# Stacked keys with doubled queries, a 128-row pool product, and the feed-forward output in groups of 2, 4, 8 and 8 tiles

## The chip, the cores and the metric

The kernel runs on one core of one Trainium2 chip. The metric is the time of one execution on the device in microseconds (us); three runs of the kernel before gave 3009.57, 3010.11 and 3011.67 us, and their median is 3010.11 us. A core has a matrix engine (PE, with its weight loads shown apart as PEld), a vector engine (DVE), a scalar engine (ACT), GpSimd (POOL) and a queue engine (SP). In this kernel SP and POOL also issue the DMA transfers.

## The reference, cut to what matters

Two layers over 1024 positions of 1024 channels. Each layer is a mixing part and a feed-forward part.

```
h    = rmsnorm(x) ; proj = h @ w_in -> q, k, v, forget logits, conv inputs, pool input px, 3 gates
qh,kh= rmsnorm per head (8 heads of 64) ; c = cumsum(log sigmoid(forget logits))
logits[t,s] = qh[t].kh[s] / 8 + c[t] - c[s], causal ; a = softmax(logits) @ v ; y_attn = a @ w_attn_out
y_conv = short_conv(...) @ w_conv_out
y_pool = per group g of 4:  d_g (64 channels) @ pool_w[g] (64 x 256), times a scale
x    = x + (g0*y_attn + g1*y_conv + g2*y_pool) @ w_o
h    = rmsnorm(x) ; gt, up = split(h @ w_ffn_in) ; x = x + (silu(gt)*up) @ w_ffn_out     (2816 hidden channels)
```

All values are float32. The kernel keeps the precision with a high and a low part for each operand, and most products take three matmuls: high by high, high by low, low by high.

## The kernel before, in words

Everything is held transposed: channels on the 128 partitions, positions along the row, in two halves of 512 positions (`n` = 0, 1). A product tile is 128 channels by 512 positions in one PSUM bank. `mm3` (lines 226 to 228) issues the three matmuls for every 128 input channels. The code is written as units in a queue (`plan`); a scheduler then sets the order of instructions of every engine from priorities and dependences, and puts in the waits. Each engine works through its list in that order.

**Attention.** Heads go in four pairs `p`; a pair's 128 channels are head `e`=0 on partitions 0 to 63 and head `e`=1 on 64 to 127. `qk_evac` and `scale_one` (lines 502 to 567) turn a product of q or k into the operands of the scores. For q of head 0 there is `qa`: the high part on rows 0 to 63, the low part on rows 64 to 127 (`qb` for head 1, mirrored). For k there are `ka` and `kb` (the high part of one head, written twice, on both halves of the rows) and `kl` (the low parts of both heads, each on its own half). `scores` (lines 648 to 684) runs over the blocks of 128 queries, `i` = 0 to 7, and both heads. A block has 128(i+1) keys, in chunks of at most 512. Each chunk takes two matmuls:

```
T.matmul(qk, lhsT=qs[:, tb],  rhs=kh[:, c0:c1],          start=True,  stop=False)   # line 669, 128 rows
T.matmul(qk, lhsT=qs[er, tb], rhs=d["kl"][er, c0:c1],    start=False, stop=True)    # line 670, 64 rows
```

DVE then adds the bias and takes the running maximum (line 676), ACT takes exp (line 681), DVE scales (line 683). One step later PE turns the block (`turn`, line 694), ACT and DVE split it into high and low (lines 697, 698), and one step after that PE multiplies by the values (line 711). Between these, `fill` puts steps of other products of `plan`: gates, and q, k and v of the next pairs. The bias rows of a pair, `negcb`, are loaded by SP (line 644) into 6 buffers, 4 per pair.

**Merge.** `merge_unit` (lines 914 to 950) makes 16 outputs of 20 matmuls per layer: 12 for attention, 6 for convolution, 2 for pooling (lines 933 and 934). The pooled input `pd` has the high part of a group on its own 64 rows and the low part on the other 64; the weight is loaded onto both halves. Line 933 multiplies all 128 rows by the weight's high part, line 934 the 64 high rows by the weight's low part.

**Feed-forward.** The 22 tiles of hidden channels are made by plain units (two tiles) and by `strassen_unit` (20 tiles), seven products of four channel tiles for each pair of tiles. Each finished tile is split into `ah` and `al` and stored to memory (lines 998, 999). The output product reads them back: `load_act` loads the tiles of a list `order` into 28 places, which are the operand tiles of the Strassen products, in the order in which those are read for the last time; each load waits until its place is free. `GROUPS` cuts the 22 tiles into three groups of 8, 8 and 6; in each group the product goes over 8 output tiles `m` and 2 halves `n`, and DVE adds the result to `x` (line 1167); the products go round seven PSUM banks (`dbank`). In group 0, `x` is loaded from memory (`load_x`, line 971, SP) just ahead of each output. `x`, `ah`, `al` and the temporaries share a ring of 18 tiles. The weights of one unit are 128 output channels wide; `load` (lines 107 to 129) brings them in on SP, ACT makes the high part (line 122), DVE the low (line 123), with 2 raw buffers and 3 split ones.

Of the kernel before, what the change touches and what calls it, by code (L numbers as in the profile page):

```python
# [9 lines left out]
F32 = mybir.dt.float32  # L10
F32R = mybir.dt.float32r
AF = mybir.ActivationFunctionType
ALU = mybir.AluOpType
# [17 lines left out]
FB = DFF // P  # L31
EPS = 1e-6
NEG = -1.0e30
GROUPS = [(0, 8), (8, 8), (16, 6)]
RING = 18
LOOK = 2
FINE = 4
# [18 lines left out]
def trunk_kernel(ctx: ExitStack, tc: tile.TileContext, x, norm_mix_g, w_in, forget_b, q_norm_g, k_norm_g,  # L56
# [158 lines left out]
    def dbank():  # L215
        tags = dense_tags[0]
        t = tags[dense_at[0] % len(tags)]
        dense_at[0] += 1
        return ps.tile([P, HN], F32, tag=t, name="dps", bufs=2 if t in ("qk", "pt") else 1)

    def mm3(dst, ws, rs, start=True, stop=True, again=False):

        n = len(ws)
        for k in range(n):
            (wh, wl), (rh, rl) = ws[k], rs[k]
            T.matmul(dst, lhsT=wh, rhs=rh, start=start and k == 0, stop=False, skip_group_check=again)  # L226
            T.matmul(dst, lhsT=wh, rhs=rl, start=False, stop=False, skip_group_check=again)  # L227
            T.matmul(dst, lhsT=wl, rhs=rh, start=False, stop=stop and k == n - 1, skip_group_check=again)  # L228
# [211 lines left out]
    for l in range(L):  # L440
# [49 lines left out]

        def pair_tiles(p):
            d = heads.setdefault(p, {})
            for nm in ("ka", "kb", "kl"):
                d[nm] = ap.tile([P, S], F32R, tag=nm, name=f"{nm}{p}", bufs=2)

        def v_tile(p):
# [49 lines left out]
        def scale_one(p, which, n, qf, r):  # L546
            d = heads[p]
            cols = slice(n * HN, (n + 1) * HN)
            gcol = (gqs if which == "q" else gk)[:, l:l + 1]
            V.scalar_tensor_tensor(out=qf, in0=qf, scalar=gcol, in1=r, op0=ALU.mult, op1=ALU.mult)  # L550
            lo, hi = slice(0, HD), slice(HD, P)
            if which == "q":
                qa = ap.tile([P, HN], F32R, tag="qa", name="qa", bufs=3)
                qb = ap.tile([P, HN], F32R, tag="qb", name="qb", bufs=3)
                A.copy(out=qa[lo], in_=qf[lo])
                A.copy(out=qb[hi], in_=qf[hi])
                V.tensor_tensor(out=qa[hi], in0=qf[lo], in1=qa[lo].bitcast(F32), op=ALU.subtract)
                V.tensor_tensor(out=qb[lo], in0=qf[hi], in1=qb[hi].bitcast(F32), op=ALU.subtract)
                d["qa", n], d["qb", n] = qa, qb
            else:  # L560
                A.copy(out=d["ka"][lo, cols], in_=qf[lo])
                A.copy(out=d["kb"][hi, cols], in_=qf[hi])
                A.copy(out=d["ka"][hi, cols], in_=qf[lo])
                A.copy(out=d["kb"][lo, cols], in_=qf[hi])
                V.tensor_tensor(out=d["kl"][lo, cols], in0=qf[lo], in1=d["ka"][lo, cols].bitcast(F32),
                                op=ALU.subtract)
                V.tensor_tensor(out=d["kl"][hi, cols], in0=qf[hi], in1=d["kb"][hi, cols].bitcast(F32),
                                op=ALU.subtract)

        v_dram = dr.tile([P, 2, KT, P], F32R, tag="vd", name="vd")  # L570

# [67 lines left out]
        def load_negc(p):  # L639
            for c in range(NH):  # L640
                for e in range(2):
                    hrow = negc_dram[2 * p + e:2 * p + e + 1, :]
                    t = ap.tile([P, HN], F32, tag="negcb", name="negcb", bufs=6)
                    nc.sync.dma_start(out=t, in_=hrow[:, c * HN:(c + 1) * HN].broadcast_to([P, HN]))
                    negc[p, e, c] = t

# [4 lines left out]
        def scores(ch):  # L651

            p, i, e = ch
            d = heads[p]
            qs, kh = (d["qa", i // 4], d["ka"]) if e == 0 else (d["qb", i // 4], d["kb"])
            tb = slice(i % 4 * P, (i % 4 + 1) * P)
            er = slice(e * HD, (e + 1) * HD)
            n_s = (i + 1) * P
            lg = ap.tile([P, S], F32, tag="lg", name="lg", bufs=3)
            mx = ap.tile([P, 6], F32, tag="mx", name="mx", bufs=4)  # L660
            nm = ap.tile([P, P], F32, tag="nm", name="nm", bufs=3)
            dg = i % 4 * P
            G.affine_select(out=nm, in_=negc[p, e, i // 4][:, dg:dg + P], pattern=[[-1, P]], compare_op=ALU.is_ge,
                            fill=NEG, base=0, channel_multiplier=1)
            top = -3.0e38
            at = 0
            for c, c0, c1 in chunks(i):
                qk = ps.tile([P, HN], F32, tag="qk", name="qk", bufs=2)
                T.matmul(qk[:, 0:c1 - c0], lhsT=qs[:, tb], rhs=kh[:, c0:c1], start=True, stop=False)  # L669
# [242 lines left out]
        def merge_unit(mm):  # L912
            specs = [wspec(w_attn_out[l], (0, 512), mm * 2 * P, 2 * P)]

            def run(w):
# [7 lines left out]
                for m in (2 * mm, 2 * mm + 1):  # L923
                    g = m // 2
                    c2 = slice(m % 2 * P, (m % 2 + 1) * P)
                    c4 = slice(m % 4 * P, (m % 4 + 1) * P)
                    rows = slice((g % 2) * HD, (g % 2 + 1) * HD)
# [41 lines left out]
        def load_x(m, n):  # L969
            xt[m, n] = ring("x")  # L970
            nc.sync.dma_start(out=xt[m, n], in_=xs[m, n])
# [182 lines left out]
        def ffo_unit(g, m, halves, before=None):  # L1154
            j0, nj = GROUPS[g]
            last = g == len(GROUPS) - 1

            def run(w):
                wh, wl = w[0]
                if before:  # L1160
                    before()
                for n in halves:
                    if g == 0:
                        load_x(m, n)
                    b = dbank()
                    mm3(b, [(wh[:, k, :], wl[:, k, :]) for k in range(nj)], [act[j0 + k, n] for k in range(nj)])
                    V.tensor_tensor(out=xt[m, n], in0=b, in1=xt[m, n], op=ALU.add)  # L1167
                    if last and l < L - 1:
                        square_acc(nq, m, n, xt[m, n])
                    yield  # L1170
            return Unit([wspec(wfo, (j0 * P, (j0 + nj) * P), m * P, P)], run)

        for n in range(NH):
            for m in range(KT):
# [32 lines left out]
        for g in range(len(GROUPS) - 1):  # L1207
            for m in range(KT):
                before = None
                if g == 0 and m == 0:  # L1210
                    before = lambda: load_act(20, 28)
                elif g == 1 and m == 0:
                    before = lambda: load_act(28, 44)
                plan.append(ffo_unit(g, m, range(NH), before))
        prefetch()
        run_tail()
        wx_stack.close()
# [63 lines left out]
```

## Time and profile before

| | |
|---|---|
| median of three runs | 3010.11 us |
| the profiled execution | 3009.41 us |
| its span, first to last instruction | 3007.6 us, mean granted clock 0.995 |
| PE busy | 2975.6 us (99%), 13680 matmuls |
| DVE busy | 1723.1 us (57%) |
| ACT busy | 1224.8 us (41%) |
| DMA | 353.83 MB, 118 GB/s over the span |

A row of the timeline gives an instruction's start and its duration. Matmuls overlap: one that lasts 0.39 us starts 0.23 us after the one before it, so the time that a matmul takes from PE is read from start to start, not from its duration. The shape "64\*128 64x512" is a matmul over 64 rows into 128 columns of weights with 512 moving columns. What stands in brackets at a row's end is idle time before it and what ended it.

### The profile page before, as it was taken

The numbers are of one execution on the slowest core, as the hardware profiler recorded it, in microseconds if no ns is written. First come the engines' busy times: TensorE is split into PE (matmuls) and PEld (weight loads), VectorE is DVE, ScalarE is ACT, GpSimd is POOL, SyncE is SP. The second block draws the span as 40 slices with busy tenths as digits, with TensorE's granted clock in tenths as the row PEclk, the third lists the DMA queues.
The fourth block names the chain that finished last, engine by engine and source line by source line (L and its number), as shares of the span: only waits on it lengthen the run. The fifth ranks groups of instructions, "written<-read, shape, count | busy, mean of one in ns | idle before, by whom it ended". The sixth has DMA issues, their size and how long they took to land.

```text
span 3007.6 us, 36474 instructions
## 1 busy us (share of the span) xinstructions
PE 2975.6 (99%) x13680; PEld 2408.9 (80%) x13680; DVE 1723.1 (57%) x3133; ACT 1224.8 (41%) x1935; POOL 426.9 (14%) x756
## 2 busy tenths in 40 slices
PE   8999999999999999999999999999999999999999
PEld 7778777887888888788887887788778888887887
DVE  7776765438585555422577667544476855653223
ACT  6666653222454444300367567432224443442002
POOL 3101111000411111321211111110003111114200
PEclk9999999999999999999999999999999999999999
DMA  5222223235533333763421231232355333338623
GB/s 170 74 77 82 73 83 105 69 107 160 189 98 112 112 112 112 231 202 115 129 84 60 74 93 63 91 116 74 107 168 176 99 112 112 110 109 266 194 63 119
DMA packets 348889, 353.83 MB, mean 118 GB/s; under 512 B 26376, under 2 KB 263432, under 8 KB 348456
## 3 DMA queue, kind: packets, MB, share of 16 engines
q1 hardware_dynamic: 281864, 208.80, 23.1%
q0 software_dynamic: 66848, 142.70, 14.7%
q8 instruction: 107, 1.75, 0.2%
q14 instruction: 70, 0.57, 0.1%
HBM read 252.81 MB, written 98.63 MB: 117 GB/s over the span
## 4 chain that ended last, share of the span: by engine, by line
PE 91%; DVE 5%; DMA 2%; issue 1%; ACT 1%; POOL 0%; SPq 0%; DVEq 0%; ACTq 0%; POOLq 0%
PE dps L226 27%; PE dps L227 26%; PE dps L228 26%; PE qk L670 2%; PE pv L711 2%; PE pt L694 2%; PE qk L669 2%; PE dps L602 1%; PE dps L604 1%; PE dps L603 1%; DVE hf L1033 1%; DVE t L232 1%; DVE hf L292 1%; DMA wr<-in_w_in_dram 1%; DMA acl<-acd 1%
## 5 line engine op out<-in xcount | busy, mean ns | idle before, releaser
L226 PE MATMUL dps<-hh,wh 128*128 128x512 f32 x1408 | 572.3, 407 | 0.0
L227 PE MATMUL dps<-hl,wh 128*128 128x512 f32 x1408 | 552.5, 393 | 1.5 <-DVE hl L232 1.1
L228 PE MATMUL dps<-hh,wl 128*128 128x512 f32 x1408 | 551.3, 392 | 0.0
L122 ACT CAST wh<-wr 128x1024 fp32r<-128x1024 f32 (+1 forms) x200 | 203.4, 1017 | 693.0 <-PE dps L227 610.1
L123 DVE TENSOR_TENSOR wl<-wr,wh 128x1024 fp32r<-128x1024 f32 (+1 forms) x200 | 240.3, 1201 | 209.6 <-ACT wh L122 209.0
L226 PEld LDWEIGHTS dps<-hh,wh 128*128 128x128 f32 x1408 | 265.7, 189 | 62.5 <-issue 12.1
L228 PEld LDWEIGHTS dps<-hh,wl 128*128 128x128 f32 x1408 | 265.3, 188 | 57.9
L227 PEld LDWEIGHTS dps<-hl,wh 128*128 128x128 f32 x1408 | 265.9, 189 | 47.3 <-DVE hl L232 1.5
L227 PE MATMUL dps<-acl,wh 128*128 128x512 f32 x704 | 277.2, 394 | 7.2 <-DMA acl<-acd 7.0
L226 PE MATMUL dps<-ach,wh 128*128 128x512 f32 x704 | 277.0, 394 | 2.7 <-DMA ach<-acd 2.6
L228 PE MATMUL dps<-ach,wl 128*128 128x512 f32 x704 | 275.8, 392 | 1.3 <-DVE wl L123 1.3
L1167 DVE TENSOR_TENSOR x<-dps,x 128x512 f32<-128x512 f32 x96 | 66.3, 691 | 333.1 <-PE dps L228 311.0
L226 PE MATMUL dps<-t,wsh 128*128 128x512 f32 x640 | 249.2, 389 | 0.0
L227 PE MATMUL dps<-t,wsh 128*128 128x512 f32 x640 | 249.0, 389 | 0.0
L228 PE MATMUL dps<-t,wsl 128*128 128x512 f32 x640 | 249.0, 389 | 0.0
L226 PE MATMUL dps<-hh,wsh 128*128 128x512 f32 x480 | 187.0, 390 | 0.9 <-ACT p L1114 0.9
L228 PE MATMUL dps<-hh,wsl 128*128 128x512 f32 x480 | 186.7, 389 | 0.0
L227 PE MATMUL dps<-hl,wsh 128*128 128x512 f32 x480 | 186.7, 389 | 0.0
L227 PEld LDWEIGHTS dps<-acl,wh 128*128 128x128 f32 x704 | 133.0, 189 | 38.6 <-DMA acl<-acd 11.7
L226 PEld LDWEIGHTS dps<-ach,wh 128*128 128x128 f32 x704 | 132.9, 189 | 34.2 <-DMA ach<-acd 7.1
L228 PEld LDWEIGHTS dps<-ach,wl 128*128 128x128 f32 x704 | 133.3, 189 | 28.8 <-DVE wl L123 1.7
L1077 DVE TENSOR_TENSOR wsl<-wr,wsh 128x1024 fp32r<-128x1024 f32 x80 | 76.2, 953 | 117.7 <-ACT wsh L1076 117.7
(263 smaller groups left out, 5461.6 us busy)
## 6 DMA issues: line engine op xcount, KB each, us to landing
wr<-in_w_in_dram SPq DMA_DIRECT2D x88, 512.0 KB, 3.8
wr<-in_w_ffn_in_dram SPq DMA_DIRECT2D x40, 1024.0 KB, 5.2
acd<-ah POOLq DMA_DIRECT2D x88, 256.0 KB, 2.3
acd<-al POOLq DMA_DIRECT2D x88, 256.0 KB, 2.5
acl<-acd POOLq DMA_DIRECT2D x88, 256.0 KB, 7.5
ach<-acd POOLq DMA_DIRECT2D x88, 256.0 KB, 7.1
td<-tg POOLq DMA_DIRECT2D x80, 256.0 KB, 2.5
tin<-td SPq DMA_DIRECT2D x80, 256.0 KB, 2.9
```

What stands on the lines that cost most here:

```text
L122: A.copy(out=hi[:, 0:cnt], in_=rv)
L123: V.tensor_tensor(out=lo[:, 0:cnt], in0=rv, in1=hi[:, 0:cnt].bitcast(F32), op=ALU.subtract)
L226: T.matmul(dst, lhsT=wh, rhs=rh, start=start and k == 0, stop=False, skip_group_check=again)
L227: T.matmul(dst, lhsT=wh, rhs=rl, start=False, stop=False, skip_group_check=again)
L228: T.matmul(dst, lhsT=wl, rhs=rh, start=False, stop=stop and k == n - 1, skip_group_check=again)
L232: eng.tensor_tensor(out=lo, in0=src, in1=hi.bitcast(F32), op=ALU.subtract)
L669: T.matmul(qk[:, 0:c1 - c0], lhsT=qs[:, tb], rhs=kh[:, c0:c1], start=True, stop=False)
L670: T.matmul(qk[:, 0:c1 - c0], lhsT=qs[er, tb], rhs=d["kl"][er, c0:c1], start=False, stop=True)
L694: T.transpose(pt[:, j * P:(j + 1) * P], lg[:, c0 + j * P:c0 + (j + 1) * P], idf)
L711: T.matmul(pv[:, e], lhsT=vs[:, j, :], rhs=pps[c][:, j - c0 // P], start=j == 0, stop=j == i)
L1077: V.tensor_tensor(out=lv, in0=src, in1=hv.bitcast(F32), op=ALU.subtract)
L1167: V.tensor_tensor(out=xt[m, n], in0=b, in1=xt[m, n], op=ALU.add)
```

## The change

Scores: for q there are now two tiles per head, `qh` (the high part on both halves of the rows) and `ql` (the low part on both halves). For k there is one tile per head: the high part on the head's own half, the low part on the other. Both matmuls of a chunk use 128 rows and the same keys; `kl` is gone, and the bias rows have 4 buffers. The second pool matmul also takes all 128 rows. The output product has four groups, of 2, 4, 8 and 8 tiles; a unit of a group has 4, 2, 1 and 1 output tiles. All loads of the first 28 tiles are asked for at once after the last `strassen_unit`; the other 16 come at three later units.

```diff
-GROUPS = [(0, 8), (8, 8), (16, 6)]
+GROUPS = [(0, 2), (2, 4), (6, 8), (14, 8)]
+OUT_COLS = {2: 4, 4: 2, 8: 1}
...
-                A.copy(out=qa[lo], in_=qf[lo])
-                A.copy(out=qb[hi], in_=qf[hi])
-                V.tensor_tensor(out=qa[hi], in0=qf[lo], in1=qa[lo].bitcast(F32), op=ALU.subtract)
-                V.tensor_tensor(out=qb[lo], in0=qf[hi], in1=qb[hi].bitcast(F32), op=ALU.subtract)
-                d["qa", n], d["qb", n] = qa, qb
-            else:
-                A.copy(out=d["ka"][lo, cols], in_=qf[lo])
-                A.copy(out=d["kb"][hi, cols], in_=qf[hi])
-                A.copy(out=d["ka"][hi, cols], in_=qf[lo])
-                A.copy(out=d["kb"][lo, cols], in_=qf[hi])
-                V.tensor_tensor(out=d["kl"][lo, cols], in0=qf[lo], in1=d["ka"][lo, cols].bitcast(F32),
-                                op=ALU.subtract)
-                V.tensor_tensor(out=d["kl"][hi, cols], in0=qf[hi], in1=d["kb"][hi, cols].bitcast(F32),
-                                op=ALU.subtract)
+            for e, (own, other) in enumerate(((lo, hi), (hi, lo))):
+                src = qf[own]
+                if which == "q":
...
+                    A.copy(out=qh[own], in_=src)
+                    A.copy(out=qh[other], in_=src)
+                    V.tensor_tensor(out=ql[own], in0=src, in1=qh[own].bitcast(F32), op=ALU.subtract)
+                    V.tensor_tensor(out=ql[other], in0=src, in1=qh[own].bitcast(F32), op=ALU.subtract)
+                    d["q", e, n] = qh, ql
+                else:
+                    k = d["ka" if e == 0 else "kb"]
+                    A.copy(out=k[own, cols], in_=src)
+                    V.tensor_tensor(out=k[other, cols], in0=src, in1=k[own, cols].bitcast(F32), op=ALU.subtract)
...
-                    t = ap.tile([P, HN], F32, tag="negcb", name="negcb", bufs=6)
+                    t = ap.tile([P, HN], F32, tag="negcb", name="negcb", bufs=4)
...
-                T.matmul(qk[:, 0:c1 - c0], lhsT=qs[:, tb], rhs=kh[:, c0:c1], start=True, stop=False)
-                T.matmul(qk[:, 0:c1 - c0], lhsT=qs[er, tb], rhs=d["kl"][er, c0:c1], start=False, stop=True)
+                T.matmul(qk[:, 0:c1 - c0], lhsT=qh[:, tb], rhs=keys[:, c0:c1], start=True, stop=False)
+                T.matmul(qk[:, 0:c1 - c0], lhsT=ql[:, tb], rhs=keys[:, c0:c1], start=False, stop=True)
...
-                        T.matmul(bq, lhsT=ql[rows, g % 2, c2], rhs=pd[g, n][rows], start=False, stop=True)
+                        T.matmul(bq, lhsT=ql[:, g % 2, c2], rhs=pd[g, n], start=False, stop=True)
...
+                for n in halves:
+                    for m in range(m0, m0 + nm):
+                        if g == 0:
+                            load_x(m, n)
+                        b = dbank()
+                        c = slice((m - m0) * P, (m - m0 + 1) * P)
+                        mm3(b, [(wh[:, k, c], wl[:, k, c]) for k in range(nj)], [act[j0 + k, n] for k in range(nj)])
...
+            return Unit([wspec(wfo, (j0 * P, (j0 + nj) * P), m0 * P, nm * P)], run)
...
-            if u == n_units - 1:
-                load_act(0, 20)
...
+        load_act(0, 28)
+        arrivals = {(1, 0): (28, 32), (2, 0): (32, 40), (2, 7): (40, 44)}
```

What stands where now, in the built programs. Lines of the changed kernel are one higher up to the scores and a few lower behind them.

On SP at the start of the output product of layer 0 the loads of the output weights (`wr`) and of `x` stand as follows. Before:

```order
L117 DMA wr<-in_w_ffn_out_dram 128x8x128 x2
L971 DMA x<-xs_7019 128x512
L971 DMA x<-xs_7393 128x512
L971 DMA x<-xs_7057 128x512
L971 DMA x<-xs_7431 128x512
L117 DMA wr<-in_w_ffn_out_dram 128x8x128
L971 DMA x<-xs_7096 128x512
L971 DMA x<-xs_7470 128x512
L971 DMA x<-xs_7135 128x512
L971 DMA x<-xs_7509 128x512
```

After:

```order
L118 DMA wr<-in_w_ffn_out_dram 128x4x256 x2
L968 DMA x<-xs_7047 128x512
L968 DMA x<-xs_7085 128x512
L968 DMA x<-xs_7124 128x512
L968 DMA x<-xs_7163 128x512
L968 DMA x<-xs_7421 128x512
L968 DMA x<-xs_7459 128x512
L968 DMA x<-xs_7498 128x512
L968 DMA x<-xs_7537 128x512
L968 DMA x<-xs_7202 128x512
L968 DMA x<-xs_7241 128x512
L968 DMA x<-xs_7280 128x512
```

In between the loads of `x` no weight load is left; the remaining five loads of `x` follow, and then two weight loads. The order of `x` goes over four output tiles of one half, then the other half.

On DVE in the first pair of layer 0, where q of the next pair is made (`qa`, `qb`, `ql` are its low parts, `wl` the low part of a weight, line 676 before and 674 after the scores' running maximum). Before:

```order
L557 TENSOR_TENSOR qa<-qf,qa 64x512
L123 TENSOR_TENSOR wl<-wr,wh 128x1024
L558 TENSOR_TENSOR qb<-qf,qb 64x512
L676 ISA lg,mx<-qk,nm,mx 128x128
L676 ISA mx 128x1
```

After:

```order
L560 TENSOR_TENSOR ql<-qf,qh 64x512
L124 TENSOR_TENSOR wl<-wr,wh 128x1024
L561 TENSOR_TENSOR ql<-qf,qh 64x512
L560 TENSOR_TENSOR ql<-qf,qh 64x512
L561 TENSOR_TENSOR ql<-qf,qh 64x512
L674 ISA lg,mx<-qk,nm,mx 128x128
L674 ISA mx 128x1
```

Two instructions of 64 by 512 have become four.

On SP in the attention of layer 0, the bias rows (`negcb`) among the weight loads; the first two rows of them are of the third pair before (second half of the keys) and then of the fourth (first half), the last of the fourth (second half). Before:

```order
L117 DMA wr<-in_w_in_dram 128x8x128 x5
L644 DMA negcb<-negc 128x512 x2
L117 DMA wr<-in_w_in_dram 128x8x128 x2
L644 DMA negcb<-negc 128x512 x2
L117 DMA wr<-in_w_in_dram 128x8x128 x5
L644 DMA negcb<-negc 128x512 x2
```

After:

```order
L118 DMA wr<-in_w_in_dram 128x8x128 x5
L642 DMA negcb<-negc 128x512
L118 DMA wr<-in_w_in_dram 128x8x128
L642 DMA negcb<-negc 128x512
L118 DMA wr<-in_w_in_dram 128x8x128
L642 DMA negcb<-negc 128x512 x2
L118 DMA wr<-in_w_in_dram 128x8x128 x5
L642 DMA negcb<-negc 128x512 x2
```

Of these, the first three rows of `negcb` are now the third pair's four loads, and the last is the fourth pair's first half: the first half's rows used to be asked for while the pair before was still being worked on, and its two loads now stand apart, a weight load between them and one behind.

## Rows read from the trace of the kernel before

**Rows 1.** The page: head, part 1 (engine, busy us, instructions).

```profile
span 3007.6 us, 36474 instructions
...
PE 2975.6 (99%) x13680; PEld 2408.9 (80%) x13680; DVE 1723.1 (57%) x3133; ACT 1224.8 (41%) x1935; POOL 426.9 (14%) x756
```

**Rows 2.** Waits of PE, whole span: who, for whom, us, times, longest.

```profile
PE dps L227 <- DMA acl<-acd: 7.0, 6, 2.2
```

**Rows 3.** Timeline of PE, a merge output's end: start us, us, engine, line, operation.

```profile
742.00 0.39 PE L933 MATMUL dps<-pd,wqh 128*128 128x512 f32 x1
742.32 0.49 PE L934 MATMUL dps<-pd,wql 64*128 64x512 f32 x1
742.74 0.50 PE L226 MATMUL dps<-mgh,wh 128*128 128x512 f32 x1
743.08 0.40 PE L227 MATMUL dps<-mgl,wh 128*128 128x512 f32 x1
```

**Rows 4.** Timeline of PE, scores of 1024 and of 128 keys.

```profile
388.57 0.39 PE L669 MATMUL qk<-ka,qa 128*128 128x512 f32 x1
...
390.50 0.39 PE L227 MATMUL dps<-hl,wh 128*128 128x512 f32 x1
...
407.69 0.22 PE L669 MATMUL qk<-ka,qa 128*128 128x128 f32 x1
...
408.44 0.40 PE L227 MATMUL dps<-hl,wh 128*128 128x512 f32 x1
```

**Rows 5.** Line 670, `qa` (`qb` alike): xcount, duration ns min/median/max, first and last start, forms.

```profile
L670 PE MATMUL qk<-kl,qa x96: 324/468/498, 91.7 to 1977.3; 64*128 64x512 f32 x48, 64*128 64x128 f32 x16, 64*128 64x256 f32 x16, 64*128 64x384 f32 x16
```

**Rows 6.** Windows: us, then busy of PE, PEld, DVE, ACT, POOL; clock, DMA, GB/s.

```profile
90.00:505.00 415.00, 415.00 (x2055) 324.96 (x2054) 282.78 (x787) 247.81 (x445) 47.67 (x107) 1.00 0.24 74
676.00:746.00 70.00, 70.00 (x284) 51.77 (x283) 61.10 (x91) 14.63 (x21) 0.00 (x0) 1.00 0.52 158
1258.00:1282.00 24.00, 20.01 (x76) 14.11 (x75) 5.68 (x7) 2.62 (x3) 11.72 (x23) 0.93 1.19 371
```

**Rows 7.** Waits of DVE between 90 and 505 us.

```profile
DVE lg L676 <- PE qk L670: 40.9, 34, 6.5
```

**Rows 8.** Groups of DVE, 90 to 505 us: busy us, mean ns, idle before.

```profile
L558 DVE TENSOR_TENSOR qb<-qf,qb 64x512 fp32r<-64x512 f32 x6 | 4.1, 688 | 0.2
```

**Rows 9.** Timeline, a turn and the DVE work it needs.

```profile
227.34 0.54 DVE L683 TENSOR_SCALAR lg<-lg,mx 128x512 f32<-128x512 f32 x1
...
227.95 0.65 PE L694 MATMUL pt<-idf,lg 128*128 128x128 f32 x4
```

**Rows 10.** Timeline, start of the output product, layer 0, then layer 1.

```profile
1258.80 0.39 PE L226 MATMUL dps<-ach,wh 128*128 128x512 f32 x1
...
1264.24 0.39 PE L226 MATMUL dps<-ach,wh 128*128 128x512 f32 x1
...
1270.96 0.69 DVE L1167 TENSOR_TENSOR x<-dps,x 128x512 f32<-128x512 f32 x1 [5.31 <-DMA x<-xs]
...
1275.61 0.69 DVE L1167 TENSOR_TENSOR x<-dps,x 128x512 f32<-128x512 f32 x1 [3.96 <-PE dps L228]
...
2750.63 0.40 PE L226 MATMUL dps<-ach,wh 128*128 128x512 f32 x1
...
2759.15 0.69 DVE L1167 TENSOR_TENSOR x<-dps,x 128x512 f32<-128x512 f32 x1 [5.33 <-DMA x<-xs]
...
2766.35 0.63 PE L227 MATMUL dps<-acl,wh 128*128 128x512 f32 x1
2766.78 0.63 PE L228 MATMUL dps<-ach,wl 128*128 128x512 f32 x1
...
2768.15 0.69 DVE L1167 TENSOR_TENSOR x<-dps,x 128x512 f32<-128x512 f32 x1 [8.30 <-PE dps L228]
```

**Rows 11.** DMA issues: line, queue, xcount, KB each, median us to landing.

```profile
x<-xs SPq DMA_DIRECT2D x64, 256.0 KB, 10.9
...
negcb<-negc SPq DMA_DIRECT2D x32, 256.0 KB, 3.4
```

More of the change, by code (lines that the diff above doesn't have):

```diff
@@ L492, in pair_tiles @@
             d = heads.setdefault(p, {})
-            for nm in ("ka", "kb", "kl"):
+            for nm in ("ka", "kb"):
                 d[nm] = ap.tile([P, S], F32R, tag=nm, name=f"{nm}{p}", bufs=2)
@@ L551, in scale_one @@
             lo, hi = slice(0, HD), slice(HD, P)
-            if which == "q":
-                qa = ap.tile([P, HN], F32R, tag="qa", name="qa", bufs=3)
-                qb = ap.tile([P, HN], F32R, tag="qb", name="qb", bufs=3)
-                A.copy(out=qa[lo], in_=qf[lo])
-                A.copy(out=qb[hi], in_=qf[hi])
-                V.tensor_tensor(out=qa[hi], in0=qf[lo], in1=qa[lo].bitcast(F32), op=ALU.subtract)
-                V.tensor_tensor(out=qb[lo], in0=qf[hi], in1=qb[hi].bitcast(F32), op=ALU.subtract)
-                d["qa", n], d["qb", n] = qa, qb
-            else:
-                A.copy(out=d["ka"][lo, cols], in_=qf[lo])
-                A.copy(out=d["kb"][hi, cols], in_=qf[hi])
-                A.copy(out=d["ka"][hi, cols], in_=qf[lo])
-                A.copy(out=d["kb"][lo, cols], in_=qf[hi])
-                V.tensor_tensor(out=d["kl"][lo, cols], in0=qf[lo], in1=d["ka"][lo, cols].bitcast(F32),
-                                op=ALU.subtract)
-                V.tensor_tensor(out=d["kl"][hi, cols], in0=qf[hi], in1=d["kb"][hi, cols].bitcast(F32),
-                                op=ALU.subtract)
+            for e, (own, other) in enumerate(((lo, hi), (hi, lo))):
+                src = qf[own]
+                if which == "q":
+                    qh = ap.tile([P, HN], F32R, tag=f"qh{e}", name="qh", bufs=3)
+                    ql = ap.tile([P, HN], F32R, tag=f"ql{e}", name="ql", bufs=3)
+                    A.copy(out=qh[own], in_=src)
[7 more added lines that the diff above has]
+                    V.tensor_tensor(out=k[other, cols], in0=src, in1=k[own, cols].bitcast(F32), op=ALU.subtract)
         v_dram = dr.tile([P, 2, KT, P], F32R, tag="vd", name="vd")
@@ L654, in scores @@
             d = heads[p]
-            qs, kh = (d["qa", i // 4], d["ka"]) if e == 0 else (d["qb", i // 4], d["kb"])
+            qh, ql = d["q", e, i // 4]
+            keys = d["ka" if e == 0 else "kb"]
             tb = slice(i % 4 * P, (i % 4 + 1) * P)
-            er = slice(e * HD, (e + 1) * HD)
             n_s = (i + 1) * P
@@ L926, in run @@
                     c4 = slice(m % 4 * P, (m % 4 + 1) * P)
-                    rows = slice((g % 2) * HD, (g % 2 + 1) * HD)
                     for n in range(NH):
@@ L1152, in load_act, with ffo_unit @@
                 act[order[t]] = (hi, lo)
-        def ffo_unit(g, m, halves, before=None):
+        def ffo_unit(g, m0, halves, arrive=()):
             j0, nj = GROUPS[g]
+            nm = OUT_COLS[nj]
             last = g == len(GROUPS) - 1
@@ L1159, in run @@
                 wh, wl = w[0]
-                if before:
-                    before()
+                if arrive:
+                    load_act(*arrive)
                 for n in halves:
[L1163 to L1171, printed above, removed]
+                    for m in range(m0, m0 + nm):
[4 more added lines that the diff above has]
+                        mm3(b, [(wh[:, k, c], wl[:, k, c]) for k in range(nj)], [act[j0 + k, n] for k in range(nj)])
+                        V.tensor_tensor(out=xt[m, n], in0=b, in1=xt[m, n], op=ALU.add)
+                        if last and l < L - 1:
+                            square_acc(nq, m, n, xt[m, n])
+                        yield
+            return Unit([wspec(wfo, (j0 * P, (j0 + nj) * P), m0 * P, nm * P)], run)
         for n in range(NH):
@@ L1204, in trunk_kernel @@
             strassen_unit(u)
-            if u == n_units - 1:
-                load_act(0, 20)
[L1207 to L1214, printed above, removed]
+        load_act(0, 28)
+        arrivals = {(1, 0): (28, 32), (2, 0): (32, 40), (2, 7): (40, 44)}
+        for g, (j0, nj) in enumerate(GROUPS[:-1]):
+            for m0 in range(0, KT, OUT_COLS[nj]):
+                plan.append(ffo_unit(g, m0, range(NH), arrivals.get((g, m0), ())))
         prefetch()
```

## The prediction, on record before the run

> **What bounds the kernel now.** I read the page's head first: PE is busy 2975.6 of 3007.6 us (99%), DVE 57%, ACT 41% [rows 1]. The waits of PE say the same from the other side: the largest one of the whole span is 7.0 us, six waits for reloaded hidden tiles [rows 2]. So a microsecond taken from PE's list is a microsecond gained, until another engine or a transfer stands where PE stood. What the list holds is read from start to start: the first output of the feed-forward output product has 24 matmuls of 512 columns, and they take 1258.80 to 1264.24 [rows 10], 5.44 us or 0.227 us each. Next I looked for matmuls that take more than that, then, in windows by stage, at how far DVE is behind PE where the change makes PE faster.
>
> **The 64-row matmuls.** In a merge output the 128-row matmul at 742.00, the 64-row one at 742.32 and two 128-row ones follow one another, the last at 743.08 [rows 3]. From 742.00 to 743.08 there are three steps, 1.08 us where three normal ones would be 0.68. One 64-row matmul costs 0.40 us beyond its own time, and the excess is spread over the step into it (0.32), the step out of it (0.42) and the next (0.34). Scores of 1024 keys have two such matmuls: 388.57 to 390.50, 1.93 us for five steps [rows 4], against 1.135; again 0.40 each. With 128 keys there are two short matmuls and one of 512 columns in the 0.75 us from 407.69 to 408.44 [rows 4]. Taking the short ones as a quarter of 0.227 the excess is 0.41; were each held to half of 0.227 it would be 0.30. I take 0.36, and 0.39 for 256 and 384 keys, which lie between.
>
> Counts: line 670 runs 192 times (96 for `qa`, as many for `qb`): 96 of 512 keys, 32 each of 384, 256 and 128 [rows 5]; line 934 runs 32 times (16 outputs in two layers). With all 128 rows in both matmuls the sum is 96 x 0.40 + 64 x 0.39 + 32 x 0.36 + 32 x 0.40 = 87.7 us, bounds 85 to 90. The number of matmuls stays.
>
> A rule of the Trainium skill speaks against this: "TensorE: Matmul & The Clock Gate", section "Why this matters for your kernels", says that a single matmul with few rows takes as long as one with 128. By it, filling the rows saves nothing, and the first rival below holds. Its page "TensorEngine Tiling (Array Packing)", section "Key Properties", says that a change of tiling mode, though not of the tile alone, drains the engine; that is the pattern of [rows 3], where 128-row matmuls behind the 64-row one are late too.
>
> **What the vector engine makes of it.** A product of q needs four subtractions of 64 x 512 instead of two. At 0.688 us each [rows 8] and 16 more per layer (four pairs, two halves, two each) that is 11.0 us per layer on DVE. ACT's copies are two more for q and two fewer for k: nothing. Between 90 and 505 us of layer 0, DVE is busy 282.8 and ACT 247.8 of 415 [rows 6]; but work and chain are not the same. Of DVE's idle time only 40.9 us is a wait for the scores [rows 7]; if none of the rest could be shortened, the window would be 415 - 40.9 + 11.0 = 385 us. PE alone would need 415 less its share of the gain: 48 x 0.40 + 32 x 0.39 + 16 x 0.36 = 37.4, so 377.6. The difference, 7.5, is the most that I let DVE take back per layer, 15 for both. The closest place is a scaling that ends at 227.88 with the turn that reads it at 227.95 [rows 9]: 0.07 us of room where scores ahead of the turn come out 0.4 to 0.8 sooner. But such a wait of half a microsecond is mostly made up, as the scores behind it are not needed at once. I take 4 us, nearer to none, since DVE has 130 us of idle time in that window; bounds 0 and 15.
>
> Merge: between 676 and 746 DVE is busy 61.1 of 70 us for 14 outputs [rows 6], 4.36 us each; PE needs 5.0 now and 4.60 then. PE stays the later one by 0.24 per output: 0, at most a quarter of the 12.8 us that PE gains on the 32 outputs, 3 us.
>
> The bias rows in 4 buffers: a pair's first load now waits for the last block of the pair before, whose scores start at 388.57; the next pair's first scores start at 407.69 [rows 4]. A load takes 3.4 us [rows 11], and 19 are there. Hidden: 0; exposed at all six changes of pair it would be 6 x 3.4 = 20, which I count with the DVE bound's rival. The weight load between the two loads waits for a split that PE's own progress allows, and delays only the second of them, whose scores come later.
>
> **The start of the output product.** Before, its second output starts on PE at 1264.24 and is added at 1275.61, 11.37 us for 24 matmuls of 5.44; in layer 1 it is 2750.63 to 2768.15, 17.52 [rows 10]. About 0.2 of it is the lag from the last matmul to the add. So 5.7 and 11.9 us are lost, 17.6 in all, as the tiles 5 to 8 arrive one by one; part of it is matmuls that come 0.43 apart (2766.35 to 2766.78). With a first group of two tiles, four loads (each high and low) are enough for 16 outputs; the first output before found eight tiles' first half in place without a stall. So this goes: -17.6. Group 1 wants its four tiles 16 x 6 x 0.227 = 21.8 us after the start, at about 1280.6, when the tiles that held up the second output had been there since 1275.
>
> What is late next is `x`. Group 0 now has 16 outputs of 1.36 us instead of 5.44, so `x` is wanted four times as fast. DVE waited 5.31 and 5.33 us for the first one, until 1270.96 and 2759.15 [rows 10], unnoticed by PE then. PE goes round seven banks; with seven outputs of 1.36 us ahead of the first add it reaches 1258.80 + 9.52 = 1268.3, and in layer 1 (2750.63 - 5.44 + 9.52) 2754.7. If the first `x` comes as before and its add takes 0.69, PE stands 3.3 and 5.1 us: 8.4. The pace behind it: 371 GB/s in 1258 to 1282 [rows 6], and if `x` has half of that, 256 KB [rows 11] every 1.41 us against 1.36, 0.8 us over 16. Against that, the two weight loads ahead of `x` come in rows twice as long, which can only bring `x` forward, and none stands between the loads of `x`. I take 4, half of 8.4; bounds 0 and 17.6 (all given back). The 16 extra adds per layer, 0.69 each, lie beside at least 1.36 us of PE each: 0.
>
> **Sum.** -87.7 + 4 - 17.6 + 4 = -97.3. The profiled execution took 3009.4 (span 3007.6 and 1.8 around it) and the median of the runs is 0.7 above it: 3010.1 - 97.3 = 2912.8, so 2913 us.
>
> **Rivals.** (A) The excess belongs to the place, not to the 64 rows (a new accumulation, a change of operands), and stays. For it: 64-row matmuls stand only where a new tile of PSUM follows. Against: products of 128 rows change tiles and banks every 24 matmuls or fewer without it; between 1258.80 and 1264.24 nothing is above 0.227 on the mean. Then only the output product gains: 3010.1 - 17.6 + 4 = 2996.5.
> (B) DVE becomes the bound of the attention, with the bias loads partly exposed: the whole 15 instead of 4, 2924; with exposed loads up to 2938. For it: 0.07 us of room [rows 9], idle time that is made of waits in a chain. Against: DVE is busy 68%, ACT 60% [rows 6].
> (C) `x` starves group 0, and the output product gains nothing: 2913 + 13.6 = 2927. For it: 371 GB/s is carried at that time, and the loads of hidden tiles compete. Against: `x` was asked for early and needs 1.41 per 1.36 us.
> (D) Slower: PE, no longer the later one, idles in the attention between steps often enough for its clock to drop to the lower level of 1.2 GHz; the matmuls of [rows 10] at 2766 are 0.43 apart instead of 0.227, after PE had waited for tiles. Place: the small blocks of each pair. Each such matmul costs 0.20 us; a quarter of the 2 x 2055 matmuls of the two attention windows [rows 6] would cost 206, 3119 us; it decides from 97.3 / 0.20, about 490 matmuls or 110 us of such work. Against: the granted clock is 1.00 in that window [rows 6], PE has plenty of other products to fill in, and it would need long waits where I see room of tenths.
>
> **How the numbers follow.** The sum 0.66; A 0.04; B 0.13; C 0.14; D 0.02; 0.01 is left for no gain at all by something that I don't see. The likeliest case's own range is 2902 (90 instead of 87.7, and none of the two times 4 lost) to 2921. B and C reach 2938; the range goes to there, which leaves out A, D and the rest, and a little below. About 0.2% (6 us) is what a measurement of this kernel can tell from no change. All cases but D and the rest are faster by more: 0.97, 0.01 within, 0.02 slower.
>
> **What would show it.** Second score matmuls 0.227 us after the first and the next 0.227 behind, merge outputs every 4.6 us: the first step. If the spacing stays at 0.32 and 0.42, A is right. Waits of PE for turns, or for `lg` and splits, between the start of the attention and its end, measure DVE's share; a granted clock below 1.00 there is D. At the output product, no waits for `acl` and `ach` in the first outputs, and waits of PE for a bank while DVE waits for `x` give the last term; over 6 us of them per layer is C. Bias loads show as DVE waits at a pair's first blocks. I am wrong if the total lies beyond 2938 or if the 64-row excess turns out to be hidden time, that is, if PE's list gets shorter by 88 us and waits take its place.

## The result and the profile after

The changed kernel takes 2907.54 us (median of four runs, 2906.62 to 2908.38) where the kernel before took 3009.84 in the same comparison: a ratio of 0.9661, interval 0.9644 to 0.9678. The forecast was 2913, the range 2900 to 2938. The profiled execution took 2906.62 us.

The head and part 1 of the page after, against [rows 1]:

```profile
span 2904.8 us, 36584 instructions
...
PE 2880.7 (99%) x13680; PEld 2405.1 (83%) x13680; DVE 1758.9 (61%) x3193; ACT 1224.7 (42%) x1931; POOL 432.7 (15%) x756
```

PE lost 94.9 us of busy time with the same 13680 matmuls; DVE gained 35.8. The end of a merge output after, against [rows 3] (start, duration, engine, line, operation):

```profile
700.53 0.39 PE L930 MATMUL dps<-pd,wqh 128*128 128x512 f32 x1
700.76 0.39 PE L931 MATMUL dps<-pd,wql 128*128 128x512 f32 x1
700.98 0.39 PE L227 MATMUL dps<-mgh,wh 128*128 128x512 f32 x1
701.21 0.39 PE L228 MATMUL dps<-mgl,wh 128*128 128x512 f32 x1
```

The second pool matmul and the two behind it now start 0.22 to 0.23 us apart. From 700.53 to 701.21 it is 0.68 us where it was 1.08. Scores of 1024 and of 128 keys after, against [rows 4]:

```profile
364.22 0.40 PE L667 MATMUL qk<-ka,qh 128*128 128x512 f32 x1
364.46 0.39 PE L668 MATMUL qk<-ka,ql 128*128 128x512 f32 x1
364.69 0.40 PE L667 MATMUL qk<-ka,qh 128*128 128x512 f32 x1
364.92 0.39 PE L668 MATMUL qk<-ka,ql 128*128 128x512 f32 x1
365.15 0.39 PE L227 MATMUL dps<-hh,wh 128*128 128x512 f32 x1
365.38 0.39 PE L228 MATMUL dps<-hl,wh 128*128 128x512 f32 x1
...
381.70 0.22 PE L667 MATMUL qk<-ka,qh 128*128 128x128 f32 x1
381.76 0.28 PE L668 MATMUL qk<-ka,ql 128*128 128x128 f32 x1
```

364.22 to 365.38 is 1.16 us, where it was 1.93; with 128 keys the second matmul follows after 0.06 us.

Windows of the same stages, against [rows 6] (columns as there), and all that PE waits for between 89 and 477 us:

```profile
89.00:477.00 388.00, 386.91 (x2097) 329.76 (x2096) 291.56 (x806) 250.69 (x451) 49.47 (x108) 1.00 0.27 81
632.00:703.00 71.00, 71.00 (x314) 58.77 (x314) 63.93 (x98) 15.05 (x21) 0.00 (x0) 1.00 0.60 182
1212.00:1236.00 24.00, 22.95 (x100) 18.18 (x99) 12.18 (x17) 4.22 (x5) 11.46 (x22) 1.00 1.17 382
```

```profile
PE pt L692 <- DVE lg L681: 0.7, 2, 0.4
PE qk L667 <- DVE mx L674: 0.2, 1, 0.2
```

The granted clock is 1.00 in all three, in the last one instead of 0.93. In the attention of layer 0 PE waits 0.9 us.

The table gives stages from the first matmul of one kind to the last of another, read from the timelines; what the first two columns differ by, with a small rest outside these stages, adds up to the gain.

| us, layer 0 / layer 1 | before | after | scores alone | groups alone | groups 6, 8, 8 |
|---|---|---|---|---|---|
| first scores start (layer 0) | 91.6 | 89.8 | 89.7 | 89.9 | 89.6 |
| first scores to last product with v | 420.6 / 420.6 | 387.3 / 387.3 | 387.3 / 387.2 | 420.6 / 420.6 | 420.6 / 420.6 |
| first to last pool matmul | 74.7 / 74.7 | 68.3 / 68.2 | 74.7 / 74.7 | 74.7 / 74.7 | 74.7 / 74.7 |
| last Strassen matmul to last of the output product | 247.9 / 257.3 | 241.0 / 247.0 | 249.5 / 255.4 | 240.9 / 247.0 | 242.3 / 251.3 |
| last of the output product to layer 1's first scores | 73.3 | 69.5 | 74.9 | 69.6 | 69.6 |

After less before: attention -66.6, merge -13.0, output product -17.2, change of layer -3.8, start -1.7, the rest -0.5: 102.8 us between the two profiled executions. The start is no part of the change: in the runs below, with the scores of before or of after, the first scores start anywhere from 89.1 to 94.0 us.

### The profile page after: what moved, and what is told of

It reads as the page before. It is cut to its first block, busy times and chain, and to the rows that moved or that the text cites. A ratio compares the mean times of both kernels' runs of the same rounds, so it can differ in the third digit from the quotient of the medians.

```text
span 2904.8 us, 36584 instructions
## 1 busy us (share of the span) xinstructions
PE 2880.7 (99%) x13680; PEld 2405.1 (83%) x13680; DVE 1758.9 (61%) x3193; ACT 1224.7 (42%) x1931; POOL 432.7 (15%) x756
## 4 chain that ended last, share of the span: by engine, by line
PE 88%; DVE 6%; DMA 2%; ACT 2%; issue 2%; POOL 0%; SPq 0%; DVEq 0%; ACTq 0%; POOLq 0%
PE dps L227 26%; PE dps L229 26%; PE dps L228 26%; PE pv L709 2%; PE pt L692 2%; PE qk L668 1%; PE qk L667 1%; PE dps L602 1%; PE dps L600 1%; PE dps L601 1%; DVE hf L1030 1%; DMA x<-xs 1%; DVE t L233 1%; DVE hf L293 0%; DVE wl L124 0%
## 5 line engine op out<-in xcount | busy, mean ns | idle before, releaser
L227 PE MATMUL dps<-hh,wh 128*128 128x512 f32 x1408 | 561.0, 399 | 0.0
L123 ACT CAST wh<-wr 128x1024 fp32r<-128x1024 f32 x196 | 206.0, 1051 | 649.4 <-PE dps L228 519.1
L124 DVE TENSOR_TENSOR wl<-wr,wh 128x1024 fp32r<-128x1024 f32 x196 | 240.6, 1227 | 199.6 <-ACT wh L123 198.4
L1167 DVE TENSOR_TENSOR x<-dps,x 128x512 f32<-128x512 f32 x128 | 87.6, 690 | 283.6 <-PE dps L229 262.1
```

What stands on the lines that cost most here:

```text
L123: A.copy(out=hi[:, 0:cnt], in_=rv)
L124: V.tensor_tensor(out=lo[:, 0:cnt], in0=rv, in1=hi[:, 0:cnt].bitcast(F32), op=ALU.subtract)
```

## The experiments

**Scores alone.** The diff's lines for `scale_one`, `scores` and the bias rows, on the kernel before; pool and groups as before.

> The kernel before with the scores part of the change alone (q doubled, keys stacked, both score matmuls over 128 rows, bias rows in 4 buffers); pool product and output product as before. Theory T (the parts add up, each in its own stage): from the first score matmul to the last product with v PE needs 387.3 us in either layer instead of 420.6, so 66.6 us in all; the merge (74.7 us from first to last pool matmul) and the output product stay; PE still waits about 2.8 us for ACT's sh at the change of layer. Total 3009.8 - 66.6 = 2943 us, or 2941.5 if the first scores start 1.7 us sooner here too. Rival U (the 3.8 us gained at the change of layer come with the scores, through weights that are fetched sooner): that wait is gone here, 2939 us.

Measured: 2942.57 us, ratio 0.9780 (0.9766 to 0.9795). The attention is that of the changed kernel to 0.1 us, and the wait at the change of layer is there, even longer:

```profile
PE npss L282 <- ACT sh L278: 4.4, 1, 4.4
```

Theory T holds, U falls. The scores' part leaves the merge as it was; the output product and the change of layer, which it doesn't touch, move by less than 2 us each.

**Groups alone.**

```diff
-GROUPS = [(0, 8), (8, 8), (16, 6)]
+GROUPS = [(0, 2), (2, 4), (6, 8), (14, 8)]
+OUT_COLS = {2: 4, 4: 2, 8: 1}
```

with the loop and the loads that go with it.

> The kernel before with the output product in groups of 2, 4, 8 and 8 alone. Theory T: from the last Strassen matmul to the last matmul of the output product 241 us in layer 0 and 247 in layer 1 (before 247.9 and 257.3), and the wait for sh at the change of layer is gone since the last group is the cause of it (another 3.8): 3009.8 - 17.2 - 3.8 = 2989 us. Rival U: the change of layer stays, 2992.6 us. Rival V (the output product gains only because the attention ends sooner or its DMA falls elsewhere): under 10 us gained, above 3000 us.

Measured: 2987.14 us, ratio 0.9928 (0.9912 to 0.9945), the stages as T said. U and V fall. The ratios of the two parts multiply to 0.971; the pool matmuls, which neither has, are 13.0 of 3009 us (0.4%), and that makes the 0.966 or 0.967 of the whole.

**Groups in the order 6, 8, 8.**

```diff
-GROUPS = [(0, 8), (8, 8), (16, 6)]
+GROUPS = [(0, 6), (6, 8), (14, 8)]
```

> The kernel before with its three groups in the order 6, 8, 8 instead of 8, 8, 6; nothing else. Theory T: the first output needs 6 hidden tiles of a half and the second 6 more, so the stall at the start of the output product shrinks but stays, from 5.7 and 11.9 us to about 2 and 5; the wait for sh at the change of layer goes, as the last group has 8 tiles: together 10 to 15 us, 2995 to 3000 us. Rival W (the wait at the change of layer went with the small first groups, not with the larger last one): it is still here with 2.8 us, and the time between the last output product and the next first score stays at 73.2 us instead of 69.5.

Measured: 2992.20 us (one run), below the expected 2995: the start of the output product got 5.6 and 6.0 us shorter, where 3.7 and 6.9 were expected from stalls that I still took for 5.7 and 11.9. Another 1.9 us is the start, which is no part of the edit. The change of layer takes 69.6 us and no wait for `sh` is left; W falls. The reason stands on DVE. The end of layer 0 before, on DVE and then on PE, and then DVE's with 6, 8, 8 (the last bracket: idle before, and what ended it):

```profile
1506.77 1.23 DVE L123 TENSOR_TENSOR wl<-wr,wh 128x1024 fp32r<-128x1024 f32 x1 [1.98 <-ACT wh L122]
1507.91 0.68 DVE L273 TENSOR_TENSOR acc<-acc,sq 128x512 f32<-128x512 f32 x1
1508.51 0.68 DVE L1167 TENSOR_TENSOR x<-dps,x 128x512 f32<-128x512 f32 x1
```

```profile
1511.45 0.61 PE L282 MATMUL npss<-sh,ones 128*128 128x512 f32 x1 [2.77 <-ACT sh L278]
```

```profile
1498.29 0.69 DVE L1167 TENSOR_TENSOR x<-dps,x 128x512 f32<-128x512 f32 x1 [2.75 <-PE dps L228]
```

Before, the last matmul of the output product starts at 1505.35 us and its add at 1508.51: the split of a weight stands ahead of it in DVE's list and waits 1.98 us for that weight. With a last group of 8 that split is done earlier, and the add follows PE's last matmul (1497.87) at once. The wait cost more than its 2.77 us: between 1511.4 and 1514.9 us the mean granted clock was 0.54, most of it the lower of the two levels (1.2 GHz), and PE's matmuls came 0.41 to 0.43 us apart; with 6, 8, 8 it is 1.00 at the same place. I had read neither in the order nor in the trace that the change moves the split.

**Two 64-row matmuls in a row.**

```diff
-T.matmul(bq, lhsT=qh[:, g % 2, c2], rhs=pd[g, n], start=True, stop=False)
+T.matmul(bq, lhsT=qh[rows, g % 2, c2], rhs=pd[g, n][rows], start=True, stop=False)
```

> The kernel before, but in the merge the first pool matmul also takes only the 64 high rows, so that two 64-row matmuls follow one another in each of 32 outputs; the product of the weight's high part with the input's low part is left out. The order of all engines and the number of matmuls stay. Theory S (the 0.40 us belong to the change from 128 rows to 64 and back): an output still has one such change, the merge stays at 74.7 us from the first to the last pool matmul of a layer, within 1 us, and the two follow each other 0.23 us apart. Theory K (every matmul over 64 rows costs 0.40 us beyond its own time): 16 x 0.40 = 6.4 us more in each layer, 81.1 us, and the two are 0.6 us apart.

Measured: 3008.75 us (one run); first to last pool matmul 75.06 us in both layers, 0.3 more than before and 6 less than K's 81.1. The timeline at the same place as [rows 3]:

```profile
739.76 0.39 PE L228 MATMUL dps<-cuh,wcl 128*128 128x512 f32 x1
740.08 0.50 PE L933 MATMUL dps<-pd,wqh 64*128 64x512 f32 x1
740.42 0.39 PE L934 MATMUL dps<-pd,wql 64*128 64x512 f32 x1
740.74 0.50 PE L226 MATMUL dps<-mgh,wh 128*128 128x512 f32 x1
741.08 0.40 PE L227 MATMUL dps<-mgl,wh 128*128 128x512 f32 x1
```

From 739.76 to 741.08 there are four steps: 1.32 us, 0.41 above 4 x 0.227. That is the excess of a single 64-row matmul before. S holds for the price, but not for its place: I had expected 0.23 us between the two, and it is 0.34. The excess is 0.09 on the step into a change and 0.11 on the next, about 0.20 us for each change of the number of rows; a lone 64-row matmul pays it twice. Why a change costs this much is not shown.

**The second low part of q by ACT, and by GpSimd.**

```diff
-V.tensor_tensor(out=ql[other], in0=src, in1=qh[own].bitcast(F32), op=ALU.subtract)
+A.copy(out=ql[other], in_=ql[own].bitcast(F32))
```

> The changed kernel, but the second copy of q's low part is made by ACT (a copy of the first) instead of by a second subtraction on DVE: DVE is relieved of two 64 x 512 instructions per product of q, 11 us in each layer's attention. Theory D (the 2.3 us per layer by which the attention gains less than its 96 second matmuls were sped up are taken by DVE, through scalings and maxima that come late for PE): from the first score matmul to the last product with v 385 to 386.5 us instead of 387.3, and fewer waits of PE for lg and mx. Rival E (they are not DVE's; the order of PE's list and ACT set them): 387.3 or more, since ACT has 11 us more per layer, up to 389.

Measured: 2910.44 us (one run); the attention 388.0 and 387.3 us, as E said. PE's waits for the scaled scores grew from 1.4 to 3.9 us over the span:

```profile
PE pt L692 <- DVE lg L681: 3.9, 8, 0.9
```

DVE had 11 us less to do per layer, and PE was not a bit sooner. That does not clear DVE: ACT, which also makes the exp that the scaling waits for, got the work instead. The changed kernel's longest wait in the attention shows it. ACT, DVE and PE there, and then ACT and PE at the same block with the copies on ACT:

```profile
208.13 0.62 ACT L679 ACTIVATE lg<-lg,mx 128x384 f32<-128x384 f32 x1
...
209.05 0.69 DVE L561 TENSOR_TENSOR ql<-qf,qh 64x512 fp32r<-64x512 f32 x1
209.77 0.16 DVE L680 RECIPROCAL mx<-mx 128x1 f32<-128x1 f32 x1
...
210.87 0.52 PE L692 MATMUL pt<-idf,lg 128*128 128x128 f32 x3 [0.43 <-DVE lg L681]
```

```profile
210.13 1.25 ACT L561 CAST ql<-ql 64x512 fp32r<-64x512 f32 x2
211.39 0.62 ACT L679 ACTIVATE lg<-lg,mx 128x384 f32<-128x384 f32 x1
...
212.90 0.52 PE L692 MATMUL pt<-idf,lg 128*128 128x128 f32 x3 [0.45 <-DVE lg L681]
```

In the changed kernel the exp is done by 208.85, but DVE works through four subtractions of q's low parts from 206.96 to 209.74 before it turns to the reciprocal and the scaling for that block. With the copies on ACT the exp itself comes behind two of them. The wait moved from one engine's list to the other's and kept its length. So the run does not decide between D and E; the trace puts this wait down to the new low parts. The other run has `G.` for `V.` in the same line.

> The changed kernel, but the second subtraction of q's low part runs on GpSimd (POOL is busy 15% of the span) instead of DVE. Theory D: the attention takes 385 to 386.5 us from the first score matmul to the last product with v. Rival E: 387.3. Third case: a GpSimd subtraction takes over 1.2 us for 64 x 512, and the first block of a pair waits for it; then over 387.5.

Measured: 2930.51 us (one run), the attention 396.5 and 393.4: the third case. Groups of POOL over the span and of DVE in the first attention (busy, mean ns):

```profile
L561 POOL TENSOR_TENSOR ql<-qf,qh 64x512 fp32r<-64x512 f32 x32 | 51.4, 1608 | 55.2 <-issue 25.3 <-ACT qh L558 19.2 <-PE qk L668 5.2
```

```profile
L560 DVE TENSOR_TENSOR ql<-qf,qh 64x512 fp32r<-64x512 f32 x12 | 17.8, 1480 | 0.2
```

GpSimd takes 1.61 us on average. DVE's own subtraction takes 1.48 instead of 0.68 us: over the span 24 of the 32 take 1.3 to 1.8 us, each of them with one of GpSimd's running beside it for 0.8 us or more, and eight keep their 0.67 to 0.69. How long GpSimd's takes with none beside it is not shown.

**x ahead of the hidden tiles.** Four, twelve and two loads of `x` are asked for early, and not again at their old place:

```diff
+        xt.clear()
+        for m in range(4):
+            load_x(m, 0)
         load_act(0, 28)
```

> The changed kernel, with four of the loads of x asked for before the loads of hidden tiles, so that on SP one weight load of group 1 no longer stands ahead of them. Theory X (what is left of the stall at the start of the output product is x, that waits behind two weight loads): the first add of group 0 comes 5 to 6 us sooner against the end of the last Strassen matmul (now 9.3 and 9.8 us behind it), PE's waits for that add (1.2 and 1.7 us) go, and the total falls by 2 to 3 us to 2905. Rival Y (the transfers are bound by the rate, 380 GB/s at that time, not by their order): the hidden tiles or a weight of group 1 come later by as much and PE waits there, total unchanged at 2907.5.

Measured: 2905.52 us (2904.72 to 2908.68), ratio 0.9658 (0.9642 to 0.9674). The total is as X said, but the waits did not go. The first adds came sooner, and PE still waited 2.9 us for an add, now one later in the group; in the profiled run, the slowest of the four (2908.68), layer 1's output product took 248.8 us. On DVE in layer 0 that add stands right behind a split that waited for its weight:

```profile
1235.19 1.23 DVE L124 TENSOR_TENSOR wl<-wr,wh 128x1024 fp32r<-128x1024 f32 x1 [4.48 <-ACT wh L123]
```

Neither theory is right as it stands. I had not yet seen this split; so twelve:

> The changed kernel with twelve instead of four of the loads of x asked for ahead; on SP the second weight load of group 1 now stands behind the twelfth load of x (with four it stood behind the eighth, and PE then waited for the ninth x). Theory X: x keeps its pace of 1.37 us from about 6 us sooner; the wait of PE for x is under 0.5 us in both layers, the output product takes 239.8 and 245.3 us from the last Strassen matmul on (changed kernel: 241.0 and 247.0), and the total is 2904.6 us, 2 to 3 below the changed kernel. Rival Y (rate, not order): the wait moves on to the thirteenth x or to a weight of group 1, total 2906 to 2908.

Measured: 2908.57 us (2906.94 to 2910.53), ratio 0.9671 (0.9657 to 0.9684); PE waited 4.6 us. DVE in layer 0:

```profile
1230.61 0.69 DVE L1167 TENSOR_TENSOR x<-dps,x 128x512 f32<-128x512 f32 x1 [0.62 <-DMA x<-xs]
1238.58 1.23 DVE L124 TENSOR_TENSOR wl<-wr,wh 128x1024 fp32r<-128x1024 f32 x1 [7.27 <-ACT wh L123]
1239.72 3.07 DVE L1167 TENSOR_TENSOR x<-dps,x 128x512 f32<-128x512 f32 x5
```

The next adds are not late for `x`: after the split at 1238.58 five go at once. DVE stood 7.27 us ahead of that split, waiting for the weight that the loads of `x` had pushed back. It is the same trap as at the change of layer. The changed kernel once more, for comparison:

> The changed kernel once more, beside the version with twelve early loads of x on the same chip. Both theories: 2907 us, between 2906 and 2909; from the last Strassen matmul to the last of the output product 241.0 and 247.0 us within 0.5 us; the time until the first score matmul differs by 1 to 2 us from one profile to the next.

Measured: 2906.83 us (2905.74 to 2907.62); 241.2 and 247.2 us for the output product. Then two early loads, which leave the weight in time:

> The changed kernel with only the first two loads of x asked for ahead: on SP they stand between the two weight loads of group 1, so that the second of these comes 2.8 us later and not 11 or 16. Theory Q (with four and twelve early loads it was DVE's list that held PE: the split of the late weight stands ahead of adds whose x had landed, and waited 4.3 to 7.3 us): now that split has its weight in time (it has 10 us of room in the changed kernel) and does not wait more than 0.5 us, PE waits for x by about 0.3 us in layer 0 and 0.8 in layer 1 instead of 1.2 and 1.7; total 1 to 2 us below the changed kernel, 2905 to 2906. Rival Y (the rate of the transfers): PE's waits for x stay at 1.2 and 1.7 us, total 2907.

Measured: 2904.48 us (2903.68 to 2906.83), ratio 0.9656 (0.9643 to 0.9669). DVE in layer 0:

```profile
1218.50 1.23 DVE L124 TENSOR_TENSOR wl<-wr,wh 128x1024 fp32r<-128x1024 f32 x1 [2.52 <-ACT wh L123]
...
1220.24 1.28 DVE L1167 TENSOR_TENSOR x<-dps,x 128x512 f32<-128x512 f32 x2
1225.60 0.69 DVE L1167 TENSOR_TENSOR x<-dps,x 128x512 f32<-128x512 f32 x1 [4.07 <-DMA x<-xs]
...
1233.04 1.21 DVE L124 TENSOR_TENSOR wl<-wr,wh 128x1024 fp32r<-128x1024 f32 x1
1234.17 0.69 DVE L1167 TENSOR_TENSOR x<-dps,x 128x512 f32<-128x512 f32 x1
```

The split at 1233.04 has no wait, nor has the one in layer 1. Read from start to start, PE waits 0 and 1.4 us for `x` (expected 0.3 and 0.8) instead of 1.2 and 1.7; the output product takes 239.7 and 246.7 us. Q holds for the split; in layer 1 most of the wait is left, for the third `x`. The median is 2.4 us below the changed kernel's in the run above, but that run was on another chip, the ranges touch and the intervals overlap: the traces, not the times, show that this version is ahead.

## Why the prediction was right, step by step

**The 64-row matmuls: right in mechanism, a little too large.** Forecast -87.7. By the sizes at single places, which follow, PE got about 35.7 us faster around the 96 second matmuls of a layer, 71.3 in both layers against 74.9; the pool matmuls gave 13.0 against 12.8. Together 84.3, just below the bounds of 85 to 90. Added up in the traces over the three steps around each second matmul, beyond 0.227 us for 512 columns, it is less: 38.2 us per layer before and 3.4 after, so 34.8. The sizes by keys: 0.39 to 0.40 for 512, 0.39 for 256 and 384 as said; 0.26 to 0.29 for 128, where I took 0.36 from bounds of 0.30 and 0.41. The lower bound was the right end.

Rival A is out: the matmuls are in the same places and the excess is gone. The Trainium skill's sentence in "TensorE: Matmul & The Clock Gate", section "Why this matters for your kernels", that a matmul with few rows takes as long as one with 128, is not refuted by this: the second of two 64-row matmuls added nothing to the excess. What costs is the change of shape, as "TensorEngine Tiling (Array Packing)", section "Key Properties", has it without a price; here it is 0.20 us for each change.

**What the attention gives back: right size, owner shown for a part.** I took 4 us of 0 to 15 for DVE. Against those sizes the attention as a whole lost 2.3 us per layer, 4.7 in both (1.5 per layer against the steps added up). Waits of PE are 0.9 us of it in layer 0 and 0.4 in layer 1. The longest, 0.43 and 0.44 us, stands in each layer behind the new subtractions on DVE, as shown with the ACT run: the kind of place that the prediction named. The rest lies in tenths where PE's list stands in another order, and what causes it is open. Rival B did not happen. The bias rows cost nothing that can be seen: neither PE nor DVE is listed as waiting for them after, only GpSimd (57.9 us in 14 waits, before 16.8 in 4), and nobody waits for GpSimd's copy of them.

**The stall of the output product: right in mechanism, two sizes off.** Forecast -17.6 + 4. No wait for hidden tiles is left, but there was more of it than I had read. I took the matmul at 1264.24 [rows 10] for the first of the second output; counted from the first output's four matmuls among the last Strassen ones and twenty behind them (1257.66 to 1261.97), it is the tenth. Added up over all steps longer than 0.227 us, the stall of before was 7.1 and 12.6 us, 19.7 in all. The waits for `x` after, layer 0, against [rows 10], DVE and then PE, and their sum:

```profile
1218.49 1.23 DVE L124 TENSOR_TENSOR wl<-wr,wh 128x1024 fp32r<-128x1024 f32 x1 [1.82 <-ACT wh L123]
...
1224.85 0.69 DVE L1167 TENSOR_TENSOR x<-dps,x 128x512 f32<-128x512 f32 x1 [4.54 <-DMA x<-xs]
1226.21 0.69 DVE L1167 TENSOR_TENSOR x<-dps,x 128x512 f32<-128x512 f32 x1 [0.67 <-DMA x<-xs]
1227.58 0.69 DVE L1167 TENSOR_TENSOR x<-dps,x 128x512 f32<-128x512 f32 x1 [0.68 <-DMA x<-xs]
1228.93 0.69 DVE L1167 TENSOR_TENSOR x<-dps,x 128x512 f32<-128x512 f32 x1 [0.65 <-DMA x<-xs]
```

```profile
1224.16 0.39 PE L229 MATMUL dps<-ach,wl 128*128 128x512 f32 x1
1225.60 0.50 PE L227 MATMUL dps<-ach,wh 128*128 128x512 f32 x1 [1.05 <-DVE x L1167]
```

```profile
PE dps L227 <- DVE x L1167: 2.6, 2, 1.5
```

The first `x` was added 9.3 us after the last Strassen matmul (1215.55), and 9.8 in layer 1, where it had been 13.5 and 14.6: it came 4 to 5 us sooner. SP asked for it 0.3 us before that matmul in both kernels; on SP only the rows of the two weights ahead of it differ, which fits, but no run changes them alone. Then the adds follow every 1.35 to 1.43 us, which half of 371 GB/s had given as 1.41. PE stood 1.2 and 1.7 us; with the slow steps behind the waits 3.8 in all, where I had 4. The same misreading put PE's start 2.0 and 1.4 us too late, so my 3.3 and 5.1 for an `x` as late as before were too low (PE's 1.2 and 1.7, with the 4.2 and 4.9 by which `x` came sooner, make 5.4 and 6.6). Two errors cancelled: that this term came out at nearly 4 is luck. So -15.9; another 1.6 is a wait for the low part of a weight (at 1497.7 us before), which stood in the trace and which the sum left out. Together -17.5, against -17.2 measured. Rival C did not happen.

**The change of layer: missed.** -3.8 us, which the sum put at nothing. My sum looked at the start of the output product and not at its end, though the last group changed too. The wait of 2.8 us for `sh` was in the trace of before. That the forecast is only 5.5 us too high is in part luck: scores and merge gave 4.1 us less than forecast with DVE's share (79.6 instead of 83.7), the output product 3.6 more (17.2 instead of 13.6), and the change of layer and the start 5.5 that no term had.

**Merge and clock: right.** PE stayed the later one with 63.9 of 71 us on DVE, and every stage of the table has a granted clock of 1.00 after, so rival D had no ground.

## What to carry to other kernels

Read matmuls from start to start and look for steps that are longer than the columns allow; a lone matmul over another number of rows among full ones is worth filling up, if the second operand can be stacked. When a list in program order holds an instruction that waits for a transfer, whatever stands behind it waits as well, even if its own data is there: before moving a load, look at which instruction consumes it and what is queued behind that. And check the end of a stage as well as its start when its pieces change size.

## What the runs showed of the hardware

- A change between 128-row and 64-row matmuls of 512 columns costs about 0.20 us (run with two 64-row matmuls: 0.09 on the step into it, 0.11 on the next); two 64-row matmuls in a row cost 0.41 us beyond their time, as much as one alone (0.40, the kernel before).
- With half of the 64 x 512 subtractions on GpSimd, those took 1.61 us each, and the same subtractions left on DVE went from 0.68 to 1.48 us in the mean of twelve (24 of 32 took 1.3 to 1.8 us).
- After PE had waited 2.77 us at the change of layer, its matmuls came 0.41 to 0.43 us apart instead of 0.227, at a granted clock of 0.54 (the kernel before, 1511.4 to 1514.9 us).
